# In the chunked scan of an RWKV-7 layer, the output product of a step is issued behind the inverse product of the other direction

## The chip, the cores and the metric

The kernel runs on one core of one Trainium2 chip. The metric is the device time of one execution in microseconds (us). A run is compared with the kernel before by the ratio of their times.

## What is computed

Two token batches (256 and 1024 tokens, 1024 channels) pass through the same two layers. Layer 0 mixes tokens with a bidirectional RWKV-7 recurrence, layer 1 with 2-D neighbourhood attention, and a squared-ReLU MLP follows each. The change lies in the recurrence. For each of 16 heads of 64 channels, in both directions:

```python
def step(S, inp):
    r_t, w_t, k_t, v_t, a_t, b_t = inp
    sa = jnp.einsum('bhvk,bhk->bhv', S, a_t)
    S = S * w_t[:, :, None, :] + sa[..., None] * b_t[:, :, None, :] + v_t[..., None] * k_t[:, :, None, :]
    return S, jnp.einsum('bhvk,bhk->bhv', S, r_t)
...
for d in range(2):
    ...
    y = y + _wkv_scan(rf, _heads(decay), k_d, vf, -kk, kk * iclr, reverse=(d == 1))
```

The sum of both directions is then normalized per head and weighted.

## The kernel before, in words

**The stages.** Layer 0's projections come first, then the preparation of the scan's operands, then the scan itself, then the dense layers, the attention and the second MLP. Most of the time goes to the dense layers; the scan takes about a fifth.

**The scan in jobs and steps.** Time is cut into chunks of 64 tokens, and a step handles one chunk of one direction for two heads at once (128 x 128 tiles). A job (`scan_job`) has 16 steps of the forward direction and 16 of the backward one; there are ten jobs. In the text, A is the forward direction, whose step i stands at time i of the job, and B the backward one, whose step i stands at i + 0.5. The stretch from A's state product to B's is called an A half, the one from B's to A's next a B half; 10A is the A half that begins with A's step at time 10.

**The order is written out by hand.** `at(t, f)` puts a piece of work f on a list with a time t in units of a step. The list is sorted by t and run in that order, and inside `tc.manual_schedule` this order is the order of the instructions in the queues of TensorE (PE), VectorE (DVE), ScalarE (ACT) and GpSimd (POOL). The times are no waits: only the order that they give counts, and each engine works its queue in order. The DMAs are issued from SyncE's queue (SP). Waits between engines follow from which tile is written and read.

**One step** (`scan_step`) consists of:

- `s0` (t - 0.12): the product `zk` x `vt` into a PSUM tile `w` (L1002; three such tiles take turns);
- `sd` (t - 0.04): POOL decays the state (L1006);
- `s1` (t): the state product into `w` (L1013), then two ACT copies `up` (L1017);
- `s2` (t + 0.333): the inverse product, `Q` x `up` into `us` (L1022), then an ACT copy into `hv` (L1024);
- `s2c` (t + 0.51): two ACT copies of `us` into `u2` (L1031);
- `s3` (t + 0.667): the state update, `lt` x `hv` into `sn` (L1036), and two DVE instructions that make the new state `S` (L1044, or L1042 after a reset), for which the next `s1` of the direction waits;
- `s4` (t + 0.717): the output product, `zb` x `u2`, on top of `w` (L1050), and its delivery into `y`: in the first eight steps of a job an ACT copy (L1053), in the last eight a DVE add (L1055).

The tile `us` exists once for both directions: `s2` of either direction writes all of it, and `s2c` reads the half that belongs to its direction.

```python
        self.ubank, self.nbank = (self.pw.tile([P, P], F32, name=nm) for nm in ("us", "sn"))
...
            us = self.ubank
            nc.tensor.matmul(us, J["Q"][:, cc].rearrange("p d t -> p (d t)"), R["up"], start=True, stop=True)
```

**What else stands in the queues.** Between the steps lies the preparation of the later chunks. In each unit of time four products of one kind are spread at the fractions 0.05, 0.1, 0.27 and 0.43: `kps` (L943) at odd times, `aps` (L807) at even ones; the text calls the third and fourth of them c2 and c3. Four transposes into `lps` (L957) follow at odd times in the B half. ACT copies these results out (L946 `zk` at 0.7 of odd times, L960 `lt` at 0.2 of even ones); DVE masks `aps` into `zb` (L809, at 0.45 of even times). The inverse matrices `Q` of the next chunks are merged by small matmuls (L893, L911) with ACT copies into `yt` (L902) and `Q` itself (L919, at 0.7 of even times). DVE also works through 31 rank-1 updates of the next job's inverses (L847 and L849, in groups at 0.47 and 0.97).

**After the steps** (`scan_post`), each half of a job's `y` is normalized by a chain of operations at `t0 + dt`: `p1` (DVE mean, L1105), `p2` (POOL), `p3a` (DVE, L1125), `p2b` (ACT squares, L1113), `p2c` (DVE, L1117), `p3` (an inverse root: DVE L1161, then ACT L1173 and L1174, then DVE L1175 to L1177), `p4` to `p5` (POOL; DVE in the last job), four PE transposes `tr` (L1144) and an ACT copy `trc` (L1149) with the store. The first half starts when B's step 11 has delivered, the second runs into the next job's steps.

Of the kernel before, what the change touches and what calls it, by code (L numbers as in the profile page):

```python
# [48 lines left out]
class Trunk:  # L49
# [714 lines left out]
    def at(self, t, f, level=3):  # L764
        self.todo.append((t, len(self.todo), f, level))
# [229 lines left out]
    def scan_step(self, at, t, J, st, d, cc, m, ch, new, end, second):  # L995
        nc = self.nc
        g, c, o = cc // 4, cc % 4, 64 * d
        R = {}

        def s0():  # L1000
            R["w"] = self.pw.tile([P, P], F32, name="w", tag="w", bufs=3)
            nc.tensor.matmul(R["w"], J["zk"][d, g][:, c, :], J["vt"][:, cc, :], start=True, stop=new)  # L1002

        def sd():
            R["sd"] = self.sp.tile([P, P], F32, name="sd", tag="sd", bufs=3)
            nc.gpsimd.tensor_tensor(out=R["sd"], in0=st["S"], in1=self.dall[:, m, d, ch:ch + 1].to_broadcast([P, P]), op=ALU.mult)  # L1006

        def s1():
            w = R["w"]
            S = None if new else st["S"]  # L1010
            R["S"] = S
            if S is not None:
                nc.tensor.matmul(w, J["ar"][d, g][:, c, :], S, start=False, stop=True)  # L1013
            up = R["up"] = self.nxt(self.r_u1)
            for e in range(2):
                es = slice(64 * e, 64 * e + 64)
                nc.scalar.copy(up[es, es], w[:64, es])  # L1017

        def s2():

            us = self.ubank
            nc.tensor.matmul(us, J["Q"][:, cc].rearrange("p d t -> p (d t)"), R["up"], start=True, stop=True)  # L1022
            hv = J["hv"]
            nc.scalar.copy(hv[0:64, cc, :], us[o:o + 64])  # L1024
            u2 = self.nxt(self.r_u2)
            R["u2"] = u2

        def s2c():
            for e in range(2):
                es = slice(64 * e, 64 * e + 64)  # L1030
                nc.scalar.copy(R["u2"][es, es], self.ubank[o:o + 64, es])  # L1031

        def s3():

            sn = self.nbank
            nc.tensor.matmul(sn, J["lt"][d, g][:, c, :], J["hv"][:, cc, :], start=True, stop=True)  # L1036
            S2 = self.nxt(self.r_s)
            for e in range(2):
                es = slice(64 * e, 64 * e + 64)
                D = self.dall[es, m, d, ch:ch + 1]  # L1040
                if R["S"] is None:
                    nc.vector.tensor_scalar(out=S2[es, es], in0=sn[es, es], scalar1=D, scalar2=None, op0=ALU.mult)  # L1042
                else:
                    nc.vector.scalar_tensor_tensor(out=S2[es, es], in0=sn[es, es], scalar=D, in1=R["sd"][es, es], op0=ALU.mult, op1=ALU.add)  # L1044
            st["S"] = S2

        def s4():
            w, y = R["w"], J["y"]

            nc.tensor.matmul(w, J["zb"][d, g][:, c, :], R["u2"], start=False, stop=True, skip_group_check=True)  # L1050
            p0 = 64 * (cc % 2)
            if not second:
                nc.scalar.copy(y[p0:p0 + 64, cc // 2, :], w[64:128, :])  # L1053
            else:
                nc.vector.tensor_tensor(out=y[p0:p0 + 64, cc // 2, :], in0=w[64:128, :], in1=y[p0:p0 + 64, cc // 2, :], op=ALU.add)  # L1055
        at(t - 0.12, s0)
        if not new and not end:
            at(t - 0.04, sd)
        at(t, s1)
        at(t + 0.333, s2)  # L1060
        at(t + 0.51, s2c)
        if not end:
            at(t + 0.667, s3)
        at(t + 0.717, s4)

    def scan_post(self, at, J, grp, last):

        nc = self.nc
        for half in range(2):
# [5 lines left out]
            for u, g in enumerate(((1, 2), (0, 3))[half]):  # L1075
                m, c0 = grp[g]
                runs.append((m, 2 * u, c0 // 2))
            t0 = (12.5, 17.496)[half]

            def view(half=half):  # L1080
                v = J["y"].rearrange("p (x b) c -> p x b c", b=2)
# [860 lines left out]
```

## Time and profile before

| | us |
|---|---|
| device time, median of 3 runs | 4417.62 |
| lowest and highest of them | 4415.73, 4423.11 |
| the profiled execution, device time | 4416.63 |
| its span, first to last instruction | 4414.8 |
| the scan's steps within it | 811 to 1654 |
| one of the middle jobs (from one 1A to the next) | 83.8 to 86.1 |

PE is the engine with the most busy time over the span (4067.2 us), DVE the next (2682.9 us). A row of the timeline gives start and duration in us, engine, line of the kernel, operation, output and inputs with shape, how many instructions were merged (a fp32 matmul of this kernel is two instructions), and in brackets the idle time before it with the engine and tile that ended it. A row of the waits gives who waited for whom: us in total, times, and the longest.

### The profile page before, as it was taken

The page shows a single profiled execution, that of the slowest core. Times are in us where ns is not written, and L with a number is a line of the kernel's source. Part 1 is how long each engine was busy: PE and PEld are TensorE (multiplying, and loading weights), DVE is VectorE, ACT ScalarE, POOL GpSimd, SP SyncE. Part 2 cuts the span into 40 slices and gives each one's busy share as a digit, 9 for nine tenths or more (in the row PEclk, how much of TensorE's full clock was granted, in tenths as well). Part 3 has the DMA queues.
Part 4 walks back from the last instruction along what each step waited for, and adds up shares of the span by engine and source line. Part 5 has one row for each costly group of instructions (what it writes and reads, how often), then busy time and mean ns, then how long its engine had stood idle before and what let it go on. Part 6 is the DMA issues. An engine that isn't in the chain of part 4 may idle for free.

```text
span 4414.8 us, 69779 instructions
## 1 busy us (share of the span) xinstructions
PE 4067.2 (92%) x25060; PEld 3365.2 (76%) x25060; DVE 2682.9 (61%) x5242; ACT 1783.1 (40%) x4705; POOL 1714.0 (39%) x1760
## 2 busy tenths in 40 slices
PE   7888989788888888999999998989998999999999
PEld 4665669677777767788888887967776888888888
DVE  7988873467777745755555556157666565555555
ACT  6764441467766773211111113255555311111111
POOL 5446662345454543422222224044445332222222
PEclk8986779899999989999999999999998999999999
DMA  3234455666565424111111112523334211111111
GB/s 123 78 102 177 160 181 149 155 148 143 146 148 140 117 75 158 58 39 39 39 39 39 39 39 85 165 66 72 77 74 146 86 35 37 39 39 39 39 39 58
DMA packets 484156, 400.27 MB, mean 91 GB/s; under 512 B 289152, under 2 KB 392480, under 8 KB 483808
## 3 DMA queue, kind: packets, MB, share of 16 engines
q1 hardware_dynamic: 447584, 328.56, 26.9%
q10 hardware_dynamic: 34416, 61.35, 3.8%
q0 software_dynamic: 1808, 5.90, 0.4%
q8 instruction: 197, 3.23, 0.3%
q14 instruction: 151, 1.24, 0.1%
HBM read 285.66 MB, written 121.24 MB: 92 GB/s over the span
## 4 chain that ended last, share of the span: by engine, by line
PE 64%; ACT 7%; DVE 6%; issue 3%; DMA 2%; POOL 2%; SPq 1%; ACTq 0%; DVEq 0%; POOLq 0%
PE ps L95 16%; PE ps L96 16%; PE ps L97 16%; PE w L1050 2%; ACT u L1031 2%; ACT u L1017 2%; PE w L1013 1%; PE us L1022 1%; PE vps L499 1%; PE vps L500 1%; PE vps L501 1%; PE w L1002 1%; PE pt L1799 1%; PE op L1857 1%; DVE tmp L847 1%
## 5 line engine op out<-in xcount | busy, mean ns | idle before, releaser
L1414 DVE TENSOR_TENSOR x<-ps,x 128x256 f32<-128x256 f32 x1488 | 814.7, 595 | 639.7 <-PE ps L97 639.4
L95 PE MATMUL ps<-ah,whi 128*128 128x512 f32 (+1 forms) x2304 | 847.6, 368 | 5.2 <-ACT whi L89 4.5
L96 PE MATMUL ps<-al,whi 128*128 128x512 f32 (+1 forms) x2304 | 829.7, 360 | 2.7 <-POOL al L1304 2.7
L97 PE MATMUL ps<-ah,wlo 128*128 128x512 f32 (+1 forms) x2304 | 827.3, 359 | 2.4 <-POOL wlo L90 2.3
L90 POOL TENSOR_TENSOR wlo<-raw,whi 128x1024 fp32r<-128x1024 f32 (+1 forms) x178 | 390.5, 2194 | 859.4 <-ACT whi L89 830.9
L95 PE MATMUL ps<-hh,whi 128*128 128x512 f32 (+1 forms) x1536 | 547.8, 357 | 13.4 <-DVE x L1414 13.4
L96 PE MATMUL ps<-hl,whi 128*128 128x512 f32 (+1 forms) x1536 | 546.7, 356 | 0.0
L97 PE MATMUL ps<-hh,wlo 128*128 128x512 f32 (+1 forms) x1536 | 546.0, 355 | 0.0
L95 PEld LDWEIGHTS ps<-ah,whi 128*128 128x128 f32 x2304 | 438.2, 190 | 85.7 <-issue 13.2
L97 PEld LDWEIGHTS ps<-ah,wlo 128*128 128x128 f32 x2304 | 437.5, 190 | 72.8 <-POOL wlo L90 3.3
L96 PEld LDWEIGHTS ps<-al,whi 128*128 128x128 f32 x2304 | 438.8, 190 | 67.7 <-POOL al L1304 3.0
L89 ACT CAST whi<-raw 128x1024 fp32r<-128x1024 f32 (+1 forms) x206 | 200.3, 972 | 710.7 <-PE ps L96 642.4
L1393 POOL TENSOR_TENSOR rl<-rl 128x512 f32<-128x512 f32 (+1 forms) x192 | 174.3, 908 | 504.6 <-PE ps L97 462.5
L95 PEld LDWEIGHTS ps<-hh,whi 128*128 128x128 f32 x1536 | 291.5, 190 | 58.9 <-DVE x L1414 16.4
L97 PEld LDWEIGHTS ps<-hh,wlo 128*128 128x128 f32 x1536 | 291.8, 190 | 41.8
L1392 ACT ACTIVATE rl<-ps 128x512 f32<-128x512 f32 (+1 forms) x192 | 100.7, 525 | 550.1 <-PE ps L97 550.1
L96 PEld LDWEIGHTS ps<-hl,whi 128*128 128x128 f32 x1536 | 291.4, 190 | 40.5
L1050 PE MATMUL w<-u,zb 128*128 128x128 f32 x640 | 158.9, 331 | 96.7 <-ACT u L1031 95.4
L1395 ACT CAST hh<-rl 128x512 fp32r<-128x512 f32 (+1 forms) x192 | 105.6, 550 | 320.6 <-POOL rl L1393 320.5
L1044 DVE SCALAR_TENSOR_TENSOR S<-sn,dall,sd 64x64 f32<-64x64 f32 x512 | 145.0, 283 | 147.0 <-PE sn L1036 133.7
L1006 POOL TENSOR_TENSOR sd<-S,dall 128x128 f32<-128x128 f32 x256 | 114.5, 447 | 260.8 <-DVE S L1044 191.1
L1050 PEld LDWEIGHTS w<-u,zb 128*128 128x128 f32 x640 | 97.8, 193 | 154.3 <-ACT u L1031 153.6
(310 smaller groups left out, 8634.7 us busy)
## 6 DMA issues: line engine op xcount, KB each, us to landing
raw<-in_w_down_dram SPq DMA_DIRECT2D x64, 512.0 KB, 3.5
raw<-in_w_up_dram SPq DMA_DIRECT2D x64, 512.0 KB, 3.5
ar<-ar_d SPq DMA_DIRECT2D x80, 256.0 KB, 3.4
bk<-bk_d SPq DMA_DIRECT2D x80, 256.0 KB, 3.3
ar_d<-ar ACTq DMA_DIRECT2D x32, 512.0 KB, 2.7
bk_d<-bk ACTq DMA_DIRECT2D x32, 512.0 KB, 3.5
bs<-tab SPq DMA_DIRECT2D x128, 96.0 KB, 3.8
v_d<-vt ACTq DMA_DIRECT2D x80, 128.0 KB, 4.1
```

Of the source, the lines that this page charges most:

```text
L89: nc.scalar.copy(hi[:, cs], raw)
L90: lo_eng.tensor_tensor(out=lo[:, cs], in0=raw, in1=hi[:, cs].bitcast(F32), op=ALU.subtract)
L95: mm(ps, sh, mh, start=first, stop=False)
L96: mm(ps, sh, ml, start=False, stop=False)
L97: mm(ps, sl, mh, start=False, stop=last)
L1006: nc.gpsimd.tensor_tensor(out=R["sd"], in0=st["S"], in1=self.dall[:, m, d, ch:ch + 1].to_broadcast([P, P]), op=ALU.mult)
L1044: nc.vector.scalar_tensor_tensor(out=S2[es, es], in0=sn[es, es], scalar=D, in1=R["sd"][es, es], op0=ALU.mult, op1=ALU.add)
L1050: nc.tensor.matmul(w, J["zb"][d, g][:, c, :], R["u2"], start=False, stop=True, skip_group_check=True)
L1392: nc.scalar.activation(r[:, :n], ps[:, :n], AF.Relu)
L1393: nc.gpsimd.tensor_tensor(out=r[:, :n], in0=r[:, :n], in1=r[:, :n], op=ALU.mult)
L1395: nc.scalar.copy(hh[:, :n], r[:, :n])
L1414: nc.vector.tensor_tensor(out=xv, in0=ps[:, :n], in1=xv, op=ALU.add)
```

## The change

Two numbers change. `s4` of a step moves from 0.717 to 0.884 after the start of the step. `s2` of the other direction stands at 0.833 and `s0` of the same direction's next step at 0.88 on this scale, so `s4` goes behind both. Because the last output product of a job's first half now stands at 12.384, the normalization of that half moves by 0.2, from 12.5 to 12.7, with all its operations from the load to `p5`; its transposes and the store keep their places, except in the last job, where they move by 0.2 too.

```diff
         at(t + 0.51, s2c)
         if not end:
             at(t + 0.667, s3)
-        at(t + 0.717, s4)
+        at(t + 0.884, s4)
...
-            t0 = (12.5, 17.496)[half]
+            t0 = (12.7, 17.496)[half]
```

The order of PE's queue from one `s1` of A to the next (`s3` of B and the products between are of the step before):

```
before: s1A c0 c1 s3B s4B c2 s2A s0B c3 s1B [lps or merges] s3A s4A s2B s0A s1A
after:  s1A c0 c1 s3B c2 s2A s0B s4B c3 s1B [lps or merges] s3A s2B s0A s4A s1A
```

At 3.72 and 7.72 of a job stand the four transposes `tr` of the job before; they too were behind `s4A` and are now ahead of it, directly ahead of `s2B`.

## The prediction

> **What bounds the kernel now.** First the stretches of the span (busy us of PE, its weight loads, DVE, ACT and POOL with their instructions, then PE's granted clock, DMA share, GB/s): the scan is 843 us, and no engine is full in it. Then its chain of waits, by line, and the waits themselves (who, for whom, us in total, times, longest).
>
> ```profile
> 811.00:1654.00 843.00, 706.66 (x7088) 609.07 (x7086) 566.92 (x1531) 590.17 (x2316) 394.32 (x636) 0.97 0.55 132
> ```
> ```profile
> by line: PE w L1050 11.5%; ACT u L1031 10.7%; ACT u L1017 10.5%; issue 8.5%; PE w L1013 7.3%; PE us L1022 7.3%; PE w L1002 5.4%; DVE tmp L847 4.7%; DVE S L1044 3.7%; PE kps L943 3.7%; DVE q L849 3.0%; PE aps L807 2.8%; ACT qq L919 2.2%; DMA
> ```
> ```profile
> PEld w L1050 <- ACT u L1031: 153.6, 296, 1.5
> ...
> PE w L1050 <- ACT u L1031: 95.4, 230, 1.3
> ...
> DVE y L1055 <- PE w L1050: 50.9, 83, 2.7
> ```
>
> The chain runs in a loop between PE and ACT: state product L1013, `up` L1017, `u2` L1031, output product L1050, back to PE. So L1050 is where PE stands idle, and it has the largest share of the chain. One A half (10A) shows the loop:
>
> ```profile
> 1203.89 0.39 PE L1013 MATMUL w<-S,ar 128*128 128x128 f32 x2
> ...
> 1204.37 0.43 ACT L1017 COPY u<-w 64x64 f32<-64x64 f32 x2 [0.24 <-PE w L1013]
> ...
> 1204.83 0.43 ACT L1031 COPY u<-us 64x64 f32<-64x64 f32 x2
> ...
> 1205.06 0.58 DVE L1044 SCALAR_TENSOR_TENSOR S<-sn,dall,sd 64x64 f32<-64x64 f32 x2 [1.12 <-PE sn L1036]
> ...
> 1205.31 0.49 PE L1050 MATMUL w<-u,zb 128*128 128x128 f32 x2 [0.36 <-ACT u L1031]
> ...
> 1205.64 0.39 PE L807 MATMUL aps<-ar,bb 128*128 128x128 f32 x2
> ...
> 1205.86 0.39 PE L1022 MATMUL us<-u,qq 128*128 128x128 f32 x2
> ...
> 1206.08 0.39 PE L1002 MATMUL w<-v,zk 128*128 128x128 f32 x2
> ...
> 1206.31 0.39 PE L807 MATMUL aps<-ar,bb 128*128 128x128 f32 x2
> ...
> 1206.53 0.39 PE L1013 MATMUL w<-S,ar 128*128 128x128 f32 x2
> ```
>
> Read the starts. A matmul behind another follows after 0.22 (1205.64 to 1205.86). The one that has waited costs 0.33 to the next start (1205.31 to 1205.64). This half lasts 2.64 us.
>
> Not every half is bound in this way. In one middle job DVE is full from 1149.9 to 1173.5 (22.32 of 23.60 us) and L1013 waits for the state:
>
> ```profile
> 1149.90:1173.50 23.60, 18.41 (x185) 15.54 (x184) 22.32 (x51) 15.39 (x61) 12.65 (x19) 1.00 0.44 112
> ```
> ```profile
> 1155.59 0.49 PE L1013 MATMUL w<-S,ar 128*128 128x128 f32 x2 [1.10 <-DVE S L1042]
> ```
>
> In these four steps (0 to 3) PE's order buys nothing. A job is thus DVE-bound in steps 0 to 3 and loop-bound in 4 to 15.
>
> **The change, part by part.** Sums are per middle job; nine such jobs are counted (seven are alike, and the three at the ends have parts of the terms).
>
> *The wait itself does not go away.* `s2` writes all of `us`, and the `u2` copies read `us`. So `s2A` may start only when `u2` of B is read: the same moment for which `s4B` waits now. After the change `s2` stands idle at 1205.31 and pays the 0.33, `s0` and `s4` follow at 0.22 each. The sum to the next L1013 is the same. That `s2`'s weights do not load ahead of such a wait I take from the weight load of L1050, which itself waited 153.6 us. Cost and gain: 0.
>
> *c2 gets ahead of the wait.* In each A half the third preparatory product (L807 at 1205.64, L943 at odd times) now stands before the idle time of 0.36 instead of behind it; it takes 0.22 and fits. The half shrinks from 2.64 to 2.42, if the state is there: at 10A S is ready at 1205.64, 0.67 before the earlier L1013. There are 12 loop-bound A halves. I leave out 4A and 8A (ACT is full, see below), 13A (a DMA, below) and 14A (`p3a` on DVE): 8 x 0.22 = **-1.76**.
>
> *The transposes get ahead of the wait too.* They stand at 7.72:
>
> ```profile
> 1192.59 0.49 PE L1050 MATMUL w<-u,zb 128*128 128x128 f32 x2 [0.34 <-ACT u L1031]
> 1192.92 0.60 PE L1144 MATMUL zps<-cst,y 128*128 128x128 f32 x4
> 1193.35 0.39 PE L1022 MATMUL us<-u,qq 128*128 128x128 f32 x2
> ```
>
> They take 0.43 of starts and fit, nearly, in the gap in front of L1050 (0.34 idle, the load before it included 0.5): **-0.41**. The other set, at 3.72, lies in the DVE-bound part: 0.
>
> *`s4` loses a cover.* In some B halves `s2` waits longer, for the merge of its `Q` on ACT, and `s4` runs under that wait now:
>
> ```profile
> PEld us L1022 <- ACT qq L919: 12.8, 49, 0.7
> ```
> ```profile
> 1187.47 0.52 ACT L919 COPY qq<-qps 32x128 f32<-32x128 f32 x2
> 1187.50 0.49 PE L1050 MATMUL w<-u,zb 128*128 128x128 f32 x2
> ...
> 1188.05 0.49 PE L1022 MATMUL us<-u,qq 128*128 128x128 f32 x2
> ```
> ```profile
> 1115.26 0.30 PEld L1013 LDWEIGHTS w<-S,ar 128*128 128x128 f32 x2 [0.17 <-DVE S L1044]
> ```
>
> Behind `s2` it costs its 0.22. 49 waits in ten jobs are five per job; one lies in the DVE-bound part, at the end of another (8.5, the last row) L1013 already waits 0.17 for S, which comes earlier with the half before: 3 x 0.22 + 0.08 = **+0.74**.
>
> *The deliveries come later.* L1050 starts 0.33 + 0.22 = 0.55 later against its `u2` (`s2` with the wait, `s0`), but no longer pays the cold share of 0.1 itself, so its result is 0.45 later. On ACT (first eight steps) the copy now comes behind `hv`; what is queued behind it is the next `up`. It ends about when `up` could start, so I take 0, with 0.07 per B half as the other end. At 3.75 it comes behind the inverse root on a full ACT:
>
> ```profile
> 1172.62 0.26 ACT L1053 COPY y<-w 64x128 f32<-64x128 f32 x1
> 1173.47 0.21 ACT L1173 ACTIVATE rqt<-rqx 128x8 f32<-128x8 f32 x1 [0.59 <-DVE rqx L1161]
> ...
> 1174.09 0.43 ACT L1017 COPY u<-w 64x64 f32<-64x64 f32 x2
> ...
> 1175.00 0.58 ACT L1149 COPY zt<-zps 128x512 f32<-128x512 f32 x1
> 1175.48 0.59 ACT L960 COPY lt<-lps 128x512 f32<-128x512 f32 x1
> ```
>
> Here it ran in a hole; behind the root it pushes `up` by its 0.26, and the two long copies after it leave no room to recover: **+0.26**. On DVE (last eight steps) the rank-1 updates and then S stand behind the add. In most halves S has more than 0.3 us to spare. Where the DVE-bound part begins there is none:
>
> ```profile
> 1149.60 0.29 DVE L1055 TENSOR_TENSOR y<-w,y 64x128 f32<-64x128 f32 x1 [2.28 <-PE w L1050]
> 1149.93 0.61 DVE L847 TENSOR_TENSOR tmp<-mt,q 128x31 f32<-128x31 f32 x1
> ```
>
> DVE waits 2.28 for exactly this product, and 23 us of bound work follow it: **+0.45**.
>
> *The normalization's 0.2.* Most of its operations keep their neighbours, since `s4` moves by as much. `p3` changes sides: Ln and Exp stood ahead of `hv` in ACT's queue (14.83) and now stand behind it, directly ahead of `up`:
>
> ```profile
> 1144.75 0.16 DVE L1161 TENSOR_SCALAR rqx<-va 128x8 f32<-128x8 f32 x1
> 1144.94 0.21 ACT L1173 ACTIVATE rqt<-rqx 128x8 f32<-128x8 f32 x1 [0.69 <-DVE rqx L1161]
> ```
>
> They wait for DVE, whose `rqx` comes behind the later add. So the add's 0.45 passes on to `up`, give or take 0.15 for the changed place of `hv`; I take **+0.4**. `p3a` in 14A stands behind the later add and ahead of S; it eats that half's 0.22 (left out above). DMAs: the load of `p1`'s half moves by 0.2 in SP's queue and keeps its landing long before `p3a`. But 13A waits for a transfer in six of the jobs (1.0 us on average), so gains just before it turn into wait:
>
> ```profile
> PE kps L943 <- DMA bdk<-bk_d: 6.1, 6, 2.3
> ```
>
> *Sum:* -1.76 - 0.41 + 0.74 + 0.26 + 0.45 + 0.4 = -0.32 us per job, x 9 = **-3 us**. From the profiled execution (4416.6 device time, 1.8 of it around the span) that gives 4413.6; the median shown is 1.0 above that execution: **4414**. About 0.2% (8.8 us) is what a measurement can tell from no change; this is inside.
>
> A rule of the Trainium skill bears on 14A. There two `p3a` take 1.66 us together beside POOL's mask product L948, and 0.96 at 1167.91:
>
> ```profile
> 1139.63 1.59 POOL L948 TENSOR_TENSOR zk<-zk,cst 128x256 f32<-128x256 f32 x2 [2.06 <-ACT zk L946]
> ...
> 1139.85 1.66 DVE L1125 TENSOR_TENSOR vt<-vt,bonus 128x256 f32<-128x256 f32 x2
> ```
> ```profile
> 1167.91 0.96 DVE L1125 TENSOR_TENSOR vt<-vt,bonus 128x256 f32<-128x256 f32 x2
> ```
>
> The Trainium skill, "SBUF — State Buffer", section "SBUF: two separate sides", says that GpSimd and a VectorE operation with two SBUF inputs lock the shared ports in turn for a whole instruction. The trace agrees as far as these rows go. By that rule `p3a`, starting 0.45 later, would meet less of L948, end up to 0.7 earlier than I assume, and give 14A its 0.22 back: 2 us in all, 4412.
>
> **The rivals.**
> - *The gains stay whole:* ACT, DVE and the transfer of 13A have more room than I grant, and all 12 c2 and both sets of transposes pay, with only the 0.74 against them: (-2.64 - 0.82 + 0.74) x 9 = -24, so 4393 (a third of it would be the edge of the forecast). For it: the idle time in front of L1050 in nearly every A half. Against it: S, ACT and the DMA are late next in the halves named. Chance 0.22.
> - *The add on DVE becomes the bound (slower):* the DVE add waits for the later L1050, and S behind it is late in the six halves of the last eight steps where other DVE work stands between (rank-1 updates at 8.5 and 9, `zb` and the mean at 12.5, `p3a` at 14, `va` at 14.5, the root at 15). Price: up to 0.45 in each, 2.7 per job, (-0.32 + 2.7) x 9 = +21: 4438, and some 4426 at half of it. It decides as soon as S ends more than about 2.36 us (2.42 less the hand-over) after the L1013 before it. In 9A the add would start 0.2 after L1013 and take 0.29, then come the updates of the two rows below (1115.45 to 1116.64, 1.2), then S with 0.58: it ends at 2.3. For it: L1055 already waits 50.9 us.
>
> ```profile
> 1115.45 0.40 DVE L847 TENSOR_TENSOR tmp<-mt,q 128x87 f32<-128x87 f32 x1
> ...
> 1116.42 0.22 DVE L849 TENSOR_TENSOR q<-q,tmp 128x60 f32<-128x60 f32 x1
> ```
>
> Against it: in most of these halves the add still has room. Chance 0.25.
> - *The change does what it says and `s2` is free:* if `s2` could run under the `u2` copies, it and `s0` would leave the loop with 0.44 (the wait's cold share then falls to `s4`); some 230 waits x 0.44 = -101, 4316. Against it: one `us` for both directions. Chance 0.03.
>
> **How the numbers follow.** Forecast 0.50, from 4409 to 4424; gains whole 0.22; add bound 0.25; `s2` free 0.03. Faster by over 0.2% is 0.22 + 0.03 = 0.25, within 0.50, slower 0.25. The range leaves out the farther part of each side: 4402 to 4428.
>
> **What would show it.** In the profile after, PE's idle time for `u2` should move from L1050 to L1022, nearly whole, less about 0.2 us per A half; L1050 should follow L1002 by 0.22. A half like 10A should last 2.42 instead of 2.64, a B half with a `Q` wait 0.22 more than now. L1055's wait should grow from 50.9 us to about 100. The DVE-bound part should begin about 0.45 later behind the step before. I am wrong if L1013's waits for S grow by more than 10 us in all (the add), or if L1022 starts before the `u2` copies end.

## The result and the profile after

The changed kernel took 4422.69 us in the median of 20 runs (4413.93 to 4433.44), the kernel before 4417.02 in 20 runs beside it (4407.88 to 4423.11). The ratio is 1.0017, 95% interval [1.0010, 1.0024]: slower by 7.5 us (4.4 to 10.6). The forecast was 3 us faster. The time lies in the stated range, and the difference within the 0.2% that was called no change; but the sign is wrong, and the interval lies wholly above 1. Two executions in the experiments below, one of the kernel before (5356 us) and one of e2_post_only (10394 us), were far slower than all others and are left out of the ratios and the means.

The scan's stretch of the profile after (busy us of PE, its weight loads, DVE, ACT, POOL with instructions; granted clock, DMA share, GB/s). The steps begin 3.4 us earlier than before (807.8, before 811.2) and end 8.1 us later (1662.0, before 1653.8); the granted clock was 0.97 and is 0.94.

```profile
811.00:1662.00 851.00, 712.23 (x7080) 627.36 (x7079) 561.57 (x1531) 585.45 (x2311) 390.96 (x633) 0.94 0.55 130
```

Its chain of waits, by line:

```profile
by line: PE us L1022 12.5%; ACT u L1031 9.3%; ACT u L1017 9.2%; issue 7.8%; DVE tmp L847 6.3%; PE w L1050 6.1%; PE w L1002 6.1%; PE w L1013 6.0%; PE kps L943 4.0%; DVE S L1044 3.8%; DVE q L849 3.6%; DMA bdk<-bk_d 3.6%; PE sn L1036 2.9%; ACT
```

And its waits (who, for whom: us in total, times, longest):

```profile
PEld us L1022 <- ACT u L1031: 114.9, 233, 2.0
DVE y L1055 <- PE w L1050: 107.8, 135, 2.5
...
PE us L1022 <- ACT u L1031: 57.5, 116, 1.8
...
PEld us L1022 <- ACT qq L919: 35.3, 50, 1.2
...
PE kps L943 <- DMA bdk<-bk_d: 9.9, 8, 2.4
...
PE w L1050 <- ACT u L1031: 0.3, 1, 0.3
```

The idle time for `u2` has gone from L1050 to L1022, as forecast: before, L1050's weight loads waited 153.6 us and its matmuls 95.4, now under 1 us each; L1022's wait 114.9 and 57.5. (The two rows count the same stalls in part and are not to be added.) Where the `Q` merge comes last the wait is now put down to it: 35.3 us of L1022's weight loads, 12.8 before. L1022 now leads the chain. L1055's wait is 107.8 us, forecast "about 100". And the half step is shorter where it was to be: 10A of job 3, where L1050 follows L1002 by 0.22 and L1013 of B comes 2.41 us after L1013 of A (2.64 before).

```profile
1115.11 0.39 PE L1013 MATMUL w<-S,ar 128*128 128x128 f32 x2
1115.33 0.61 PE L807 MATMUL aps<-ar,bb 128*128 128x128 f32 x4
1115.78 0.39 PE L1036 MATMUL sn<-hv,lt 128*128 128x128 f32 x2
1116.00 0.39 PE L807 MATMUL aps<-ar,bb 128*128 128x128 f32 x2
1116.53 0.49 PE L1022 MATMUL us<-u,qq 128*128 128x128 f32 x2
1116.85 0.39 PE L1002 MATMUL w<-v,zk 128*128 128x128 f32 x2
1117.07 0.39 PE L1050 MATMUL w<-u,zb 128*128 128x128 f32 x2
1117.30 0.39 PE L807 MATMUL aps<-ar,bb 128*128 128x128 f32 x2
1117.52 0.39 PE L1013 MATMUL w<-S,ar 128*128 128x128 f32 x2
```

So where does the time go? From one 1A to the next, jobs 3 and 6 lose no clock in either profile and last 82.8 and 83.8 us, 1.1 and 0.9 less than before. Job 4 lasts 89.0, 4.2 more. Four windows of 3.41 us in job 4 of the profile after:

```profile
1208.45:1211.86 3.41, 3.02 (x51) 2.48 (x49) 2.08 (x5) 2.56 (x11) 1.44 (x3) 1.00 0.76 161
1211.86:1215.28 3.42, 1.52 (x11) 1.37 (x12) 1.00 (x5) 1.89 (x9) 1.40 (x2) 1.00 0.64 162
1215.28:1218.69 3.41, 3.41 (x18) 3.41 (x18) 0.86 (x3) 0.26 (x1) 0.40 (x1) 0.51 0.82 223
1218.69:1222.10 3.41, 3.04 (x24) 2.66 (x24) 1.89 (x5) 2.75 (x11) 1.76 (x3) 0.99 1.18 164
```

In the second, PE is busy for 1.52 of 3.42 us, because L943 waits for a transfer at 13A. In the third its clock is 0.51, and matmuls start every 0.43 us instead of every 0.22:

```profile
1212.99 0.39 PE L1013 MATMUL w<-S,ar 128*128 128x128 f32 x2
1214.91 0.78 PE L943 MATMUL kps<-ar,bdk 128*128 128x128 f32 x4 [1.53 <-DMA bdk<-bk_d]
1215.49 0.64 PE L1036 MATMUL sn<-hv,lt 128*128 128x128 f32 x2
1215.92 0.63 PE L943 MATMUL kps<-ar,bdk 128*128 128x128 f32 x2
1216.34 0.63 PE L1022 MATMUL us<-u,qq 128*128 128x128 f32 x2
```

The clock falls to a half in such stretches of 3.41 us or a multiple of it. From 820 to 1625 us, counted in units of 3.41 us, there are 5 of them in the profile before and 23 in that after. The clock lost (the missing share of the clock, summed over the time) in jobs 0 to 8 is 8.5 us before and 34.8 after; these jobs last 753.2 and 763.3 us.

### The profile page after: what moved, and what is told of

Its sections match the earlier page's. It is cut to its first block, busy times and chain, and to the rows that moved or that the text cites. A ratio compares the mean times of both kernels' runs of the same rounds, so it can differ in the third digit from the quotient of the medians.

```text
span 4417.3 us, 69895 instructions
## 1 busy us (share of the span) xinstructions
PE 4056.7 (92%) x25060; PEld 3367.4 (76%) x25060; DVE 2678.4 (61%) x5242; ACT 1780.9 (40%) x4705; POOL 1716.6 (39%) x1760
## 4 chain that ended last, share of the span: by engine, by line
PE 63%; DVE 7%; ACT 6%; DMA 3%; issue 3%; POOL 2%; SPq 1%; ACTq 0%; DVEq 0%; POOLq 0%
PE ps L95 16%; PE ps L96 16%; PE ps L97 16%; PE us L1022 2%; ACT u L1031 2%; ACT u L1017 2%; DVE tmp L847 1%; PE w L1002 1%; PE w L1050 1%; PE w L1013 1%; PE vps L499 1%; PE vps L500 1%; PE vps L501 1%; PE op L1857 1%; PE pt L1799 1%
## 5 line engine op out<-in xcount | busy, mean ns | idle before, releaser
L1022 PE MATMUL us<-u,qq 128*128 128x128 f32 x640 | 161.9, 337 | 94.7 <-ACT u L1031 57.5
L1006 POOL TENSOR_TENSOR sd<-S,dall 128x128 f32<-128x128 f32 x256 | 113.8, 445 | 276.8 <-DVE S L1044 200.1
L1022 PEld LDWEIGHTS us<-u,qq 128*128 128x128 f32 x640 | 102.1, 200 | 151.4 <-ACT u L1031 114.9
```

## The experiments

Theory CLOCK: the new order gains about what was forecast, and loses it again because PE is granted half its clock more often, behind windows in which it has little to do. Rivals: ORDER (the new order itself costs the time, at an unchanged clock) and POST (the normalization's shift by 0.2 does). In the table each ratio is to the kernel before as run beside it, the clock is the mean of the granted clock over the runs of each kernel, and the last column is an estimate: the change of time (ratio less 1, times 4416 us) at an unchanged clock, with 2.2 us for each 0.001 of clock. That price is read from the runs of the kernel before alone: in four sets of its runs its time falls by 2.2, 2.2, 2.4 and 2.0 us per 0.001 of its clock from run to run. A remainder is good to some 4 us, the width of the ratios' intervals. For the changed kernel itself the clock of before is taken as 0.9530.

| kernel | ratio, 95% interval | clock | clock of before | at the same clock, us |
|---|---|---|---|---|
| the change | 1.0017 [1.0010, 1.0024] | 0.9482 | 0.9530 | -3 |
| e1_s4_only | 1.0011 [1.0002, 1.0019] | 0.9486 | 0.9530 | -5 |
| e2_post_only | 0.9996 [0.9987, 1.0005] | 0.9530 | 0.9530 | -2 |
| e3_after_fill | 0.9995 [0.9987, 1.0004] | 0.9532 | 0.9530 | -2 |
| e4_before_fill | 0.9996 [0.9988, 1.0005] | 0.9556 | 0.9530 | +4 |
| e5_c2_ahead | 0.9972 [0.9963, 0.9982] | 0.9517 | 0.9536 | -17 |
| e6_after_c2_behind | 1.0038 [1.0024, 1.0051] | 0.9506 | 0.9536 | +10 |
| e7_c2_fill | 0.9956 [0.9943, 0.9968] | 0.9544 | 0.9536 | -18 |
| e8_before_thin | 1.0012 [1.0003, 1.0021] | 0.9495 | 0.9536 | -4 |
| e9_late_0_3 | 1.0000 [0.9990, 1.0010] | 0.9520 | 0.9526 | -1 |
| e10_late_4_15 | 1.0002 [0.9993, 1.0011] | 0.9490 | 0.9526 | -7 |
| e11_late_4_15_fill | 0.9980 [0.9972, 0.9989] | 0.9530 | 0.9526 | -8 |
| e12_late_4_14 | 1.0011 [1.0000, 1.0021] | 0.9500 | 0.9532 | -2 |

The traces bear the last column out without that price. Take each half step of jobs 2 to 8 only where no clock is missing (from 2 us before it to its end), take the mean, add up a job and multiply the difference to the kernel before by 9: the change gives -3 us, e5_c2_ahead -14, e6_after_c2_behind +12, e7_c2_fill -19, e4_before_fill +4, e10_late_4_15 -3, and all thirteen lie within some 6 us of the column.

They also tie the clock to how full PE is. Slide a window of 3.41 us at full clock over the scan: PE is busy for less than 0.60 of it at 2% of the positions in the kernel before, at 4% after the change and in e8_before_thin, at under 0.5% in e4_before_fill and e7_c2_fill. Over all fourteen kernels this share and the change of the mean clock go together, with a correlation of -0.9.

**e1_s4_only**: the later output product without the normalization's shift (0.08 is needed, since the mean must follow the last product).

```diff
-        at(t + 0.717, s4)
+        at(t + 0.884, s4)
...
-            t0 = (12.5, 17.496)[half]
+            t0 = (12.58, 17.496)[half]
```

> The output product moves as in the change; the normalization starts at 12.58 instead of 12.7, so that its root keeps its place ahead of hv in ScalarE's queue. Theory CLOCK (the loss of the change comes from stretches of 3.4 us at half clock, of which the scan has some 24 instead of 5; the order of the queue by itself gains 3 to 9 us): the moved product alone makes them, so 1.001 to 1.0025, and again more than 12 such stretches. Theory POST (the shift of the normalization makes the loss, through ScalarE's root ahead of up): 0.998 to 1.000. Theory ORDER (the queue order itself is longer, above all through the add on VectorE): 1.0015, with few stretches at half clock.

4418.93 us, beside 4416.07 for the kernel before. The clock is nearly as low as with the whole change (0.9486, 0.9482), with 16 windows of half clock from 820 to 1625 us: as CLOCK expected.

**e2_post_only**: the normalization's shift alone.

```diff
-            t0 = (12.5, 17.496)[half]
+            t0 = (12.7, 17.496)[half]
```

> Only the normalization moves to 12.7; the output product stays at 0.717. CLOCK and ORDER: 0.9995 to 1.0005, at most 8 stretches at half clock. POST: 1.001 to 1.002.

4414.31 us and the clock of before, with 8 windows of half clock: the shift costs nothing that can be measured, and POST falls.

**e3_after_fill** and **e4_before_fill**: the changed kernel and the kernel before, with some of PE's products done twice or more, so that its gaps are filled. The results stay the same. The repeats in the first product of steps 1A, 2A, 2B and 3A:

```diff
-            nc.tensor.matmul(R["w"], J["zk"][d, g][:, c, :], J["vt"][:, cc, :], start=True, stop=new)
+            [nc.tensor.matmul(R["w"], J["zk"][d, g][:, c, :], J["vt"][:, cc, :], start=True, stop=new or q > 0) for q in range({(0, 1): 4, (0, 2): 2, (1, 2): 3, (0, 3): 2}.get((d, int(t)), 0) if first > 1 else 0, -1, -1)]
```

Besides, one of four `aps` and `kps` products and two of four transposes into `lps` are done twice.

> The changed kernel with products issued twice or more on TensorE where it stands idle: c1 of every group twice, two of the four transposes twice, and the vt product two to five times ahead of the state products of steps 1 to 3 that wait for S. The result is the same, only TensorE has less idle time. CLOCK: fewer than 6 stretches at half clock in the scan, and the gain of the order shows: 0.997 to 0.9995 of the kernel before. ORDER: added work gains nothing, 1.0015 to 1.004.

> The kernel before with the same repeated products. CLOCK: its five stretches at half clock go, worth 1 us each: 0.998 to 1.0005, and slower than the changed kernel with the same filling by 3 to 10 us. ORDER: 1.000 to 1.002, faster than the changed kernel with the filling.

4414.65 and 4413.45 us, beside 4416.07. With more work, the changed kernel goes from 1.0017 to 0.9995 of the kernel before, and its clock from 0.9482 to 0.9532. In the kernel before the clock rises too (0.9530 to 0.9556) and the time hardly moves: at the same clock the fill costs about 4 us there. Both ratios are as CLOCK expected, with 7 and 1 windows of half clock (under 6, and none, were expected). But it also expected the filled kernel before to be 3 to 10 us slower than the filled changed one, and the two are equal in time; they are too near each other to tell the order's gain.

**e5_c2_ahead**: the gains alone. The output product stays, and c2 and the transposes go ahead of it.

```diff
-            for c, dt in enumerate((0.05, 0.1, 0.27, 0.43, 0.45)):
+            for c, dt in enumerate((0.05, 0.1, 0.21, 0.43, 0.45)):
...
-            for c, (dt, dl) in enumerate(((0.05, 0.55), (0.1, 0.57), (0.27, 0.6), (0.43, 0.62), (0.7, 1.2))):
+            for c, (dt, dl) in enumerate(((0.05, 0.55), (0.1, 0.57), (0.21, 0.6), (0.43, 0.62), (0.7, 1.2))):
...
-            e = 0.0 if last else (19.72, 23.72)[half] - t0 - 5.809
+            e = 0.0 if last else (19.705, 23.705)[half] - t0 - 5.809
```

> The kernel before, with the output product left where it was, but with the third preparatory product (c2) and the four transposes moved ahead of it in PE's queue: the two gains of the change alone, without its costs. If each c2 ahead of the wait pays its 0.22 in 8 of the A halves of a job and the transposes pay 0.41, and PE's clock stays at its mean of 0.953: (8 x 0.22 + 0.41) x 9 = 20 us less than the kernel before, about 4396. Theory CLOCK (the change lost its gain through more stretches of half clock, which come from windows of 3.41 us in which PE is little used, where the output product was moved): the clock stays at 0.952 to 0.954 and the 20 us show nearly whole, 4394 to 4402. Rival GAINS (the gains are not there, another wait takes their place): 4412 to 4418 at an unchanged clock. Rival SPEED (any order that shortens the loop-bound halves brings the clock down): a mean clock of 0.950 or lower, and 4402 to 4412.

4401.67 us, beside 4413.86: 12 us faster, and 17 at the same clock, of 20 expected. So ORDER falls as far as these two terms go: they are there and nearly as large as worked out. But the clock fell by 0.0019 here as well, which CLOCK, as it was put (only where the output product was moved), did not expect; a part of what SPEED expected is seen.

**e6_after_c2_behind**: the changed kernel with c2 behind the wait again.

```diff
-            for c, dt in enumerate((0.05, 0.1, 0.27, 0.43, 0.45)):
+            for c, dt in enumerate((0.05, 0.1, 0.382, 0.43, 0.45)):
...
-            for c, (dt, dl) in enumerate(((0.05, 0.55), (0.1, 0.57), (0.27, 0.6), (0.43, 0.62), (0.7, 1.2))):
+            for c, (dt, dl) in enumerate(((0.05, 0.55), (0.1, 0.57), (0.382, 0.6), (0.43, 0.62), (0.7, 1.2))):
```

> The changed kernel with c2 moved behind the inverse product and the next step's first product, so that it stands behind the wait for u2 again, as before the change. If c2's place was the gain: 0.22 in 8 to 10 A halves of a job, 9 jobs, 16 to 20 us slower than the changed kernel, 4436 to 4442 at its clock of 0.948. Theory CLOCK adds that longer halves in the loop-bound part do not bring the clock back. If c2's place pays nothing (rival GAINS): 4418 to 4424. If speed itself brings the clock down (rival SPEED): a mean clock of 0.952 or higher and 4428 to 4434.

4429.63 us. At the same clock it is 13 us slower than the changed kernel (+10 against -3), where 16 to 20 were worked out from 0.22 per half; the half steps of 5A, 6A, 7A, 9A, 10A and 11A show 0.22 to 0.23 each. The time lies in SPEED's range and below CLOCK's, since the clock came part of the way back: it is 0.0030 under the kernel before, where the change was 0.0048 under. Neither theory fits alone: the longer halves did bring some clock back, but this kernel is slower than the one before and has the lower clock all the same.

**e7_c2_fill**: e5_c2_ahead with the fill of e3_after_fill.

> The kernel of e5_c2_ahead with the repeated products of e3_after_fill and e4_before_fill. Theory CLOCK: the mean clock rises by 0.002 to 0.003 against e5_c2_ahead, worth 4 to 6 us, less the 3 us that the repeated products seemed to cost: 0 to 3 us below e5_c2_ahead, about 4394 to 4400. If PE's clock has nothing to do with how full PE is: the clock of e5_c2_ahead and 3 us above it.

4396.62 us, 0.9956 [0.9943, 0.9968] of the kernel before. It is the fastest of all; against e5_c2_ahead the clock rose by 0.0027, as expected, and the time fell by 5, where 0 to 3 were expected; the two intervals overlap a little. Jobs 0 to 8 lose 1.7 us of clock (18.8 in e5_c2_ahead).

**e8_before_thin**: the kernel before with work left out: the first products of steps 1 to 3. The output lacks what they add.

```diff
-            nc.tensor.matmul(R["w"], J["zk"][d, g][:, c, :], J["vt"][:, cc, :], start=True, stop=new)
+            if new or not 1 <= int(t) <= 3: nc.tensor.matmul(R["w"], J["zk"][d, g][:, c, :], J["vt"][:, cc, :], start=True, stop=new)
...
-                nc.tensor.matmul(w, J["ar"][d, g][:, c, :], S, start=False, stop=True)
+                nc.tensor.matmul(w, J["ar"][d, g][:, c, :], S, start=not new and 1 <= int(t) <= 3, stop=True)
```

> The kernel before without the first product of a step (zk x vt) in steps 1, 2 and 3 of each job (those that do not begin a state): six matmuls of 0.22 us per job are left out, in the part that is bound by DVE, so that the output lacks what they add. Nothing else is changed. Theory CLOCK: less PE work in windows that are already little used; 8 to 20 more stretches of half clock at 1.05 us each, the mean clock 0.003 to 0.005 lower, and the kernel is slower by 5 to 15 us although it does less: 4421 to 4431. Rival (the clock does not follow from how full PE is): the same clock, and 4408 to 4416, no slower than before.

4418.53 us, beside 4413.86: slower by 0.12% [0.03, 0.21] with less to do, at a clock 0.0041 lower. This is the plainest test, since no instruction was moved to another place. The scan of its profile, to be set against the first row of the prediction (7088 instructions of PE, clock 0.97):

```profile
811.00:1654.00 843.00, 704.87 (x6954) 610.75 (x6955) 568.75 (x1527) 585.36 (x2299) 391.74 (x632) 0.95 0.55 131
```

The loss of about 5 us is at the lower edge of what CLOCK expected (5 to 15 us). By the last column the work left out gave some 4 us back; the half steps at full clock don't show that (+2), so the size is open. At the start of the DVE-bound part PE's busy share of a window goes from 1.89 of 3.40 us in the kernel before to 1.67 in this one:

```profile
1153.70:1157.10 3.40, 1.89 (x13) 1.49 (x12) 3.18 (x10) 1.39 (x8) 1.49 (x2) 1.00 0.34 77
```
```profile
1153.70:1157.10 3.40, 1.67 (x11) 1.26 (x10) 3.18 (x10) 1.37 (x7) 1.46 (x2) 1.00 0.36 77
```

The next three ask where in a job the clock is lost. **e9_late_0_3** has the output product late in steps 0 to 3 alone, **e10_late_4_15** in steps 4 to 15 alone (with the shift by 0.2), and **e11_late_4_15_fill** is e10_late_4_15 with the fill.

```diff
-        at(t + 0.717, s4)
+        at(t + (0.884 if t < 4 else 0.717), s4)
```
```diff
-        at(t + 0.884, s4)
+        at(t + (0.884 if t >= 4 else 0.717), s4)
```

> The kernel before with the output product late (0.884) in steps 0 to 3 of a job alone, the part that is bound by DVE. From the half steps of a quiet job in the traces of before and after, those of steps 0 to 4 are together 0.9 us longer after the change: x 9 = 8 us at an unchanged clock, 4422 beside 4414. Theory CLOCK: about ten of the stretches of half clock that the change added come behind a window in steps 0 to 3, so they are here too: a mean clock of 0.949 to 0.951 (before 0.953), worth 4 to 8 us more, 4426 to 4430. Rival (the clock falls because the loop-bound part became faster, and the time in steps 0 to 3 is nothing): the clock of before and 4414 to 4422.

> The changed kernel with the output product at its old place (0.717) in steps 0 to 3 of a job, late in steps 4 to 15 alone. From the half steps of a quiet job, those of steps 4 to 15 are 2 us shorter after the change: x 9 = 18 us at an unchanged clock. Theory CLOCK: the DVE-bound windows are as before, the mean clock is 0.951 to 0.953, and 4396 to 4402 beside 4414. Rival (the faster loop-bound part is what lowers the clock): a mean clock of 0.949 or lower and 4404 to 4412.

> e10_late_4_15 with the repeated products of e7_c2_fill. If the fill works as it did there, the mean clock is 0.002 to 0.003 above e10_late_4_15 and the time 4 to 6 us lower: 4392 to 4398, beside 4396.6 for e7_c2_fill. If the clock doesn't follow from the fill: no lower than e10_late_4_15.

4420.81, 4421.85 and 4411.26 us, beside 4419.64. The place that CLOCK named was wrong: steps 0 to 3 cost next to no clock (0.9520 against 0.9526) and no time that can be measured, and most of the loss of clock comes with steps 4 to 15 (0.0036 of the 0.0048). That is the rival's clock; the gain in time which both forecasts for e10_late_4_15 had did not show. The fill gives the clock back there (0.9530) and 0.22%, some 10 us, more than the 4 to 6 expected. The thinnest windows at the start of the DVE-bound part of job 4, in e9_late_0_3 and then in e10_late_4_15, say what happens:

```profile
1156.20:1159.60 3.40, 2.14 (x43) 1.63 (x41) 3.21 (x10) 1.87 (x9) 1.45 (x3) 0.99 0.20 41
```
```profile
1155.30:1158.70 3.40, 1.31 (x10) 1.03 (x9) 3.18 (x10) 1.08 (x6) 1.56 (x2) 1.00 0.36 77
```

PE is busy for 2.14 and 1.31 us of 3.40 (1.89 before): what is late in step 15 thins out the windows of step 0, where PE waits for DVE; what is late in step 0 puts a product into the gap. That called for the last run.

**e12_late_4_14**: late in steps 4 to 14 alone (with the shift by 0.2).

```diff
-        at(t + 0.884, s4)
+        at(t + (0.884 if 4 <= t < 15 else 0.717), s4)
```

> The output product late in steps 4 to 14 alone; in step 15, as in steps 0 to 3, at its old place, so that the DVE-bound part begins as before. In e10_late_4_15 most of the windows of 3.41 us with a PE share below 0.60 lie at step 0, 4.8 of them in the scan, against 1.9 before and 0.3 in e9_late_0_3. Theory START (these thin windows come from what step 15 hands over late or early): they are down to about 2, the mean clock is within 0.001 of the kernel before in the same call, and the time is 6 to 12 us below it (the half steps of 4 to 14 are 0.9 to 1.4 us shorter per job). Rival SPEED (the faster loop as a whole lowers the clock): the clock stays 0.003 to 0.004 below that of before, and the time is within 3 us of it, as in e10_late_4_15.

4419.81 us, beside 4413.86. START was right about the windows and wrong about the clock and the time. Windows at full clock with a PE share under 0.60 (counted at all positions, in units of one window, by the step in which they start) are back to 1.6 at step 0 (1.9 before, 4.8 in e10_late_4_15). But at steps 12 and 14 there are 2.3 and 1.3 of them (0.9 and none before), the clock stays 0.0032 down, as SPEED said, and the time is 5 us up, more than SPEED said. The other place of lost clock seems to be the wait for the transfer at 13A, at which a faster loop arrives earlier and waits longer.

Nor does it take a late output product to make the windows at step 0: e5_c2_ahead, which leaves it in its place, has 3.8 of them, and e6_after_c2_behind, which has it late and c2 behind the wait, has 4.3. Each of the two moves makes them; e12_late_4_14 takes both back where step 0 begins.

## Why the prediction was wrong

- **The wait stays, at another place: right.** Idle time of L1050 became idle time of L1022, the cold start with it.
- **c2 and the transposes ahead of the wait: right.** -2.17 per job times 9 is -20 us; e5_c2_ahead has them alone and shows -17 at the same clock. There c2 pays in 11 A halves of a quiet job instead of 8, but some of it is waited for again in 0B, 3B, 4A and 13A. The transposes give 0.44, forecast 0.41.
- **The costs of the later output product: near in sum, not one by one, and so in part by luck.** 1.85 per job were forecast, 17 us; the change less e5_c2_ahead is 14 at the same clock (-3 against -17). The figures that follow are medians of jobs 2 to 8 at full clock. The lost cover of the `Q` merge is 0.2 in each of 4B, 6B, 8B and 12B, against e5_c2_ahead: 0.8, forecast 0.74. The half of 15A is 0.17 shorter than before, and 0.42 shorter in e1_s4_only, where the inverse root stays ahead of `hv`: 0.25 of the 0.4. The halves 3B, 4A and 4B together grew by 0.7, and as much in e5_c2_ahead, so little of that is the delivery's 0.26. The +0.45 where the DVE-bound part begins is nearly nothing: from 15B's state product to that of 1A it takes 7.91, and took 7.87. The add does start 0.5 later against 15B, but the L847 behind it took 0.61 (the row at 1149.93 in the prediction) and now takes 0.2; why is not shown:

```profile
1144.54 0.29 DVE L1055 TENSOR_TENSOR y<-w,y 64x128 f32<-64x128 f32 x1 [2.12 <-PE w L1050]
1144.87 0.21 DVE L847 TENSOR_TENSOR tmp<-mt,q 128x31 f32<-128x31 f32 x1
```

- **14A: wrong.** It was left out as eaten by `p3a`, at no change. It lasts 0.13 longer instead, and 14B 0.10, at full clock: S comes directly behind the later add and `p3a`, and L1013 of 14B waits for it (job 3 of the profile after):

```profile
1134.39 0.29 DVE L1055 TENSOR_TENSOR y<-w,y 64x128 f32<-64x128 f32 x1 [0.72 <-PE w L1050]
...
1134.72 1.50 DVE L1125 TENSOR_TENSOR vt<-vt,bonus 128x256 f32<-128x256 f32 x2
...
1136.23 0.58 DVE L1044 SCALAR_TENSOR_TENSOR S<-sn,dall,sd 64x64 f32<-64x64 f32 x2
...
1136.87 0.49 PE L1013 MATMUL w<-S,ar 128*128 128x128 f32 x2 [0.20 <-DVE S L1044]
```

  By the Trainium skill, "SBUF — State Buffer", section "SBUF: two separate sides", `p3a` was to end up to 0.7 earlier. It takes 1.50 here and took 1.66 before: the sign agrees, the size is not enough. (Nor is the prediction's 0.96 at 1167.91 `p3a` by itself: POOL's L1006 runs beside it, from 1168.03 for 0.57.)
- **The sum of -3 us: right at the clock of the kernel before, and wrong as a time.** This is the step that failed. The sum takes every duration from the profile before and counts PE's idle time as free room, so it holds PE's granted clock at what it was. The clock fell from 0.9530 to 0.9482, which at 2.2 us per 0.001 is worth 10.6 us by estimate; the forecast -3 and 10.6 make 7.6, and 7.5 was measured. The row of the prediction's first fence had the clock of 0.97 in it, and nothing was made of it.
- **The rivals.** "The add on DVE becomes the bound" has the sign and nearly the time of its half price, but not the mechanism. L1013's waits for S did grow by more than the 10 us that were to decide (from 52.7 to 70.7 us with weight loads and matmuls added up, which counts the same stalls twice in part; from 21.1 to 29.3 for the matmuls alone). But that test was badly chosen: in e5_c2_ahead, where no add is later, the same sum is 72.3, since shorter halves arrive earlier at the same state. Some 12 of the 18 us lie in steps 0 to 4; in the last eight steps the waits at 14B grew most, by 4.8 us in ten jobs, which is this rival at one of its six places. The gains did not stay whole, and `s2` was not free.

What is shown and what is not: that the clock costs the time is shown by work left out (e8_before_thin, slower) and by work added (e3_after_fill and e11_late_4_15_fill, faster than the same kernels without it; between e7_c2_fill and e5_c2_ahead the intervals overlap). That the thin windows of step 0 come from the order around its beginning is shown by e10_late_4_15 and e12_late_4_14; but taking them back won next to no clock (0.0036 down, then 0.0032), so they alone do not explain the loss. That the earlier arrival at 13A makes the others rests on traces alone: L943's waits for its transfer are 8.2 to 11.1 us in the change, e1, e5, e10 and e12, 6.1 to 6.8 in the kernel before, e2 and e9, and 4.0 in e6, whose A halves are the long ones; an earlier transfer was not tried. One profile holds one of many positions of the windows against the jobs, so the shares of the single places are not settled.

## What to carry to other kernels

Where a stage has stretches in which PE is little more than half busy, its idle time is not free: before a sum of gains is believed, look at the windows of some 3.4 us around the stage's longest waits and ask whether the change makes them emptier. A product that fills a gap can be worth more than its own time, and work pulled ahead of a wait that another engine or a transfer ends makes the gap longer. If the time moves against a sum whose every term is seen in the trace, compare the granted clocks first.

## What the runs showed of the hardware

The half clock comes in stretches of 3.41 us or multiples, each behind a window of the same length with a low share of PE. In the profile after, the 20 windows at full clock directly ahead of one at half clock had PE shares of 0.28 to 0.70, and no window under 0.56 stayed without. There is no sharp limit: in the profiles of other kernels the shares ahead of a half clock reach 0.76 (e1_s4_only, 994.77 to 998.18), and windows down to 0.46 passed (e6_after_c2_behind, 964.59 to 968.00). One such stretch costs about 1 us of a job here, by estimate: job 4 has four of them and lasts 4.2 us longer. The chain is made of ACT's work too, which keeps its speed: one `up` copy (L1017) takes 0.204 us on average at half clock and at full clock.

The Trainium skill, "TensorE: Matmul & The Clock Gate", section "What's actually happening", gives the half rate and a free-running window of 3413 ns; the trace agrees (0.51 in 3.41 us). Its section "HAM oscillation — how this bites in real kernels" states as the rule that PE should have no idle gap over about 3.4 us. Here the measurement differs: the gap ahead of the half clock at 1215.28 was 1.53 us long, in a window in which PE was busy for 1.52 of 3.42 us.
